# A hybrid MLA and mLSTM layer: the start reordered, sums and products moved from GpSimd to VectorE, the gates' product and two staging tiles moved

## The chip, the cores and the metric

The kernel runs on one core of a Trainium2 chip. The metric is the device time of one execution in microseconds (us). The engines are PE (TensorE, the matrix unit), DVE (VectorE), ACT (ScalarE), POOL (GpSimd) and SP (SyncE, which here only issues transfers). Each engine works through its own list of instructions in order; semaphores make it wait for others.

## The reference

One layer of a diffusion backbone over 128 context and 1024 latent tokens (1152 in all), 1024 features. Cut to what the change touches:

```python
mod = silu(cond) @ w_mod + b_mod              # six vectors: sh1, sc1, gt1, sh2, sc2, gt2
h   = rmsnorm(x, g_norm_mix) * (1 + sc1) + sh1
z   = h @ w_in                                # zq, zkv, zkpe, zmq, zmk, zmv, zgate, zmo, zbr
ckv, kpe = rmsnorm(zkv, g_kv_norm), rope_2d(zkpe)
ig, lf   = zgate + b_gates, log_sigmoid(...)  # input and forget gates of the mLSTM
hm  = bidirectional_mlstm(zmq, zmk, zmv, ig, lf) ; hm = rmsnorm(hm) * sigmoid(zmo)
out = (sigmoid(g_a) * (mla(zq, ckv, kpe) @ w_o_mla) + sigmoid(g_b) * (hm @ w_o_mlstm)) @ w_out
x   = x + gt1 * out ; x = x + gt2 * swiglu(rmsnorm(x) * (1 + sc2) + sh2)
```

Inputs, weights and outputs are fp32.

## The kernel before

Every product is made of three passes in a rounded fp32 format: an operand is split into a high part (ACT, `hi`, L69) and the rest (DVE, `lo`, L75), and `mm3` (L98 to L100) adds high·high, high·low and low·high in PSUM. The big projections use Strassen's seven products in place of eight (`pair`); the sums of weight quarters that these need are made by `w_ops` on the engine `self.G`, the sums of results by `add` (L1716) on DVE. One product of a pair is 24 matmuls of 288 columns.

The instructions are put in order by a scheduler that runs its own timeline; what the code fixes are the data, the buffers, the hints `issue_after`, and how generators are interleaved: `push` appends one, and each product of a pair calls `tick`, which lets it run on to its next `yield`.

The stages that the change touches, with their times in the profiled execution:

- `start` (0 to 155 us). It loads x, the first half of the modulation weights (`wm`, four blocks) and the weights of the mLSTM values (`wv`). `gemv` makes scale and shift of a block; `square` and `stats` make each token's 1/rms, which `stats` spreads to `rbc`; `modk` scales, shifts and splits two features blocks of x. Before that is possible, three of nine token chunks of the value projection V are made from raw x (`rawmm`, L471, in full fp32, which the trace shows as two passes each), with 1/rms and the shift put right afterwards (`shift`, `spread`, L496). Then the other chunks of V follow in groups GA, GB, GC (`vmm`, 512 columns). `copy4` copies the token chunk that straddles two tiles. `t_ops` makes the four differences of x tiles that the Strassen products need.
- `z_lat` and `z_qk` (155 to 345 us): seven pairs. After the second `z_qk`, the generators `krope` and `gates` are pushed: `gates` is a long chain of small instructions on 100 rows (DVE, ACT, and two small PE products, the first at L803).
- `z_big` (345 to 616 us): twelve pairs; their results stand in tiles `zo`, get a sigmoid and are stored to `d_z`. Beside them runs `background`, the second half of the modulation: 64 times one multiply-and-accumulate (DVE, L722), one multiply (L723) and one accumulation (ACT, L704).
- From 616 us `proj` (which needs the tiles `lh`/`ll`, split by the generator `lat_kv` out of loaded pieces `wl`, and stage tiles `st`), then the mLSTM with its loads `neg`, `N`, `S`, `V`, `Q`.

Tiles are taken from numbered places (`slot`, `M`): a new tile in a place must wait until the old one has been used up, its stores included.

Of the kernel before, what the change touches and what calls it, by code (L numbers as in the profile page):

```python
# [10 lines left out]
F32 = mybir.dt.float32  # L11
# [45 lines left out]
class K:  # L57
# [231 lines left out]
    def inputs(self):  # L289

        es = contextlib.ExitStack
        rb, ps, mm = es(), es(), es()
        self.q = []
        self.stores = []
        self.arB = rb.enter_context(self.pool("arB", side="right"))
        for i in range(14):
            self.slot(i, [P, 4, GT], "r")
        self.w2 = es()
        self.wp = self.w2.enter_context(self.pool("w"))
        self.wb = (4, 4)  # L300
        self.G = self.nc.gpsimd
        self.ub = 5
        pp = self.pp = ps.enter_context(self.tc.tile_pool(name="ps1", bufs=1, space=PSUM, reuse_waits="tile"))
        with self.pool("b12") as bp:
            self.hop = {"B12": (bp.tile([P, 4, GT], R32, name="b12h"), bp.tile([P, 4, GT], R32, name="b12l"))}
            with self.pool("s0") as vp:
                self.start(vp)
        self.sp = mm.enter_context(self.pool("u"))
        self.mp = mm.enter_context(self.pool("m"))
        x = lambda nm, g: tuple(t[:, :, g * HT:(g + 1) * HT] for t in self.hop[nm])  # L310
        self.z_lat(x)
        bg = es()
# [12 lines left out]
        bg.close()  # L325
        rb.close()
        ps.close()
        self.z2(mm)

    def start(self, vp):  # L330
# [6 lines left out]
        shs = sp.tile([P, KD, 32], F32, name="shs")  # L337
# [4 lines left out]
        nc.gpsimd.memset(shs, 0.0)  # L342
# [20 lines left out]
        def gemv(b):  # L363
# [16 lines left out]
            nc.vector.tensor_copy(shs[:, 2 * b:2 * b + 2, 0:1], self.mod1[:, 2 * b:2 * b + 2, 1:2])  # L380
# [27 lines left out]
        def stats():  # L408
# [5 lines left out]
            yield r  # L414
# [31 lines left out]
        def copy4(k, j):  # L446
            for e in range(2):
                nc.gpsimd.tensor_copy(c4[:, e, k, 64 * j:64 * j + 64],
                                      self.hop[f"B{k // 4 + 1}{j + 1}"][e][:, k % 4, 0 if j else GT - 64:64 if j else GT])
# [14 lines left out]
        def rawmm(b, sw, e):  # L464

            w = sw.rearrange("p (k f) -> p k f", k=2)
            k = 2 * b + e
            for c in GR:
                if k == 0:
                    ps[c] = self.bank(pp, "mm")  # L470
                nc.tensor.matmul(ps[c], xv(k, 0)[:, c * P:(c + 1) * P], w[:, e], start=k == 0, stop=k == KD - 1)  # L471

        shv = sp.tile([P, 512], F32, name="shv")

        def shift(b):

            g = self.bank(pp, "mx")
            for e in range(2):
                nc.tensor.matmul(g[32 * e:32 * e + 32], shs[:, 2 * b + e], raw[b][:, 512 * e:512 * e + 512], start=True, stop=True)
            if b == 0:  # L480
                nc.scalar.copy(shv[0:64], g[0:64])
            else:
                nc.vector.tensor_add(shv[0:64], shv[0:64], g[0:64])

        def spread():

            sel = sp.tile([64, P], F32, name="selr")
            nc.vector.tensor_scalar(sel, self.ones[0:64], self.vec[0:64, self.V_SEL:self.V_SEL + 1], None, op0=ALU.mult)
            b = self.bank(pp, "mx")
            nc.tensor.matmul(b, sel, shv[0:64], start=True, stop=True)  # L490
            nc.scalar.copy(shv, b)

        def vout(hp, c, r=None, sh=None):
            vs = vp.tile([P, 2 * DV], F32, name=self.nm("vs"), tag="vs", bufs=3)
            if r is not None:
                nc.vector.scalar_tensor_tensor(vs, ps[c], r[:, c:c + 1], sh, op0=ALU.mult, op1=ALU.add)  # L496
            elif c % 2:
                nc.vector.tensor_copy(vs, ps[c])
            else:
                nc.scalar.copy(vs, ps[c])  # L500
            nc.sync.dma_start(self.d_v[c, :, 2 * hp:2 * hp + 2, :], vs.rearrange("p (h v) -> p h v", h=2))
        for b in range(4):
            block(b)
            vload(b)
            xload(b)
        for b in range(4):
            gemv(b)
            sw = f32v(self.wp.tile([P, 4 * DV], R32, name=self.nm("ws"), tag="wo", bufs=self.wb[1]))
            for e in range(2):
                k = 2 * b + e  # L510
                nc.scalar.activation(sw[:, 512 * e:512 * e + 512], raw[b][:, 512 * e:512 * e + 512], AF.Copy, scale=self.A1[:, k, 1:2])
# [7 lines left out]
            raw.pop(b)  # L519
            vload(b + 4)  # L520
        spread()
        for _ in st:
            pass
        for k in range(4):
            modk(k, 1)
        for c in GR:
            vout(0, c, r, shv)
        loadv(4)
        for k in range(4, KD):
            modk(k, 1)  # L530
        c4 = self.slot(13, [P, 2, KD, P], "c4")
        for i in range(4, 12):
            if i > 4:
                vload(i + 3)
            loadv(i + 1)
            for k in (2 * (i % 4), 2 * (i % 4) + 1):
                if i < 8:
                    modk(k, 0)
                    copy4(k, 0)
                    copy4(k, 1)  # L540
                for c in order[i][1]:
                    vmm(wv[i], c, k)
            if i % 4 == 3:
                for c in order[i][1]:
                    vout(1, c)
# [123 lines left out]
    def z_big(self, p, x):  # L669
# [4 lines left out]
        def dst(g):  # L674
            z[g] = self.M((0, 1)[g] if p % 2 else (3, 5)[g], [P, 2, 2, HT], "zo")
# [12 lines left out]
    def background(self):  # L688
# [17 lines left out]
        for i in range(32):  # L706
# [8 lines left out]
            for n in range(2):  # L715
# [7 lines left out]
                nc.gpsimd.tensor_tensor(w[:, n], w[:, n], sr[:, 1], op=ALU.mult)  # L723
# [7 lines left out]
    def krope(self):  # L731
# [17 lines left out]
    def gates(self):  # L749
# [781 lines left out]
    def merge(self):  # L1531
# [43 lines left out]
        self.G = nc.vector  # L1575
# [575 lines left out]
```

## Time and profile before

| what | value |
|---|---|
| three runs | 2160.06, 2153.62, 2159.26 us, median 2159.26 |
| the profiled execution | 2159.8 us, span 2158.0 us |
| granted PE clock, mean of the span | 0.974 |
| busy | PE 95%, DVE 71%, ACT 44%, POOL 24% |
| busy PE of 350 to 600 us | 243.9 of 250 |

PE is the engine that bounds the whole: what counts is where it stands still or does work that could be left out. Three places do so before 650 us: the time until the first product of V with modulated x (65.9 us), the wait in the gates (6.0 us), and the start of `proj` (9.7 us). In the rows, a time is from the span's start; what stands in brackets is the engine's idle time before the instruction and what ended it.

### The profile page before, as it was taken

What the parts mean: (1) busy time and instruction counts of PE and PEld (TensorE: products, weight loads), DVE (VectorE), ACT (ScalarE), POOL (GpSimd) and SP (SyncE); (2) the same over time, 40 slices, a digit from 0 to 9 for tenths busy, and PEclk for the clock granted to TensorE, in tenths of its full rate; (3) what the DMA queues carried; (4) which work ended last, traced back from release to release, by engine and by line L of the source; (5) the groups of instructions that cost most, each with busy time, mean ns of one, the idle gap of its engine ahead of it and who ended that gap; (6) DMA issues with size and microseconds to landing.
All of it is one profiled execution on the core that took longest, in us unless ns stands there. A gap on an engine that the chain in (4) does not pass through costs nothing.

```text
span 2158.0 us, 36478 instructions
## 1 busy us (share of the span) xinstructions
PE 2045.8 (95%) x13495; PEld 1863.7 (86%) x13495; DVE 1540.5 (71%) x3017; ACT 945.6 (44%) x1874; POOL 522.5 (24%) x413
## 2 busy tenths in 40 slices
PE   7899989999989987999999999999999999999997
PEld 3689989989978874666776799999999999999997
DVE  3846756989835878566566476998677766799896
ACT  4533334455445554333443234565323222466564
POOL 0632223667524413344446300000000000000000
PEclk9999999999989998899999999999999999999999
DMA  8332334555479776222225465324555421468664
GB/s 315 105 118 85 115 91 156 171 163 187 147 257 319 250 229 212 68 85 75 69 80 134 128 217 167 123 100 147 188 188 181 157 86 68 140 219 258 220 217 140
DMA packets 233793, 343.87 MB, mean 159 GB/s; under 512 B 20079, under 2 KB 166735, under 8 KB 232463
## 3 DMA queue, kind: packets, MB, share of 16 engines
q1 hardware_dynamic: 225070, 331.88, 47.9%
q0 software_dynamic: 4848, 6.06, 1.1%
q10 hardware_dynamic: 3696, 3.61, 0.5%
q8 instruction: 106, 1.74, 0.3%
q14 instruction: 73, 0.59, 0.1%
HBM read 253.69 MB, written 87.80 MB: 158 GB/s over the span
## 4 chain that ended last, share of the span: by engine, by line
PE 55%; DVE 10%; DMA 9%; issue 3%; ACT 2%; POOL 1%; SPq 1%; DVEq 0%; ACTq 0%; POOLq 0%
PE mm L98 14%; PE mm L100 14%; PE mm L99 13%; PE pv L1477 3%; DMA pr<-w_fo 3%; PE st L98 2%; DVE wo L75 2%; PE st L99 1%; PE st L100 1%; PE mx L1399 1%; DVE sm L1401 1%; DMA wr<-d_w 1%; PE p L1103 1%; POOL wm L723 1%; PE p L1108 1%
## 5 line engine op out<-in xcount | busy, mean ns | idle before, releaser
L98 PE MATMUL mm<-th,wo 128*128 128x288 f32 x1840 | 547.6, 298 | 6.3 <-DVE uu L1716 3.1
L100 PE MATMUL mm<-th,wo 128*128 128x288 f32 x1840 | 542.2, 296 | 4.5 <-DVE wo L75 4.5
L99 PE MATMUL mm<-tl,wo 128*128 128x288 f32 x1840 | 544.9, 296 | 0.0
L98 PEld LDWEIGHTS mm<-th,wo 128*128 128x128 f32 x1840 | 347.3, 189 | 9.1 <-issue 5.0
L100 PEld LDWEIGHTS mm<-th,wo 128*128 128x128 f32 x1840 | 347.3, 189 | 5.9 <-DVE wo L75 5.8
L99 PEld LDWEIGHTS mm<-tl,wo 128*128 128x128 f32 x1840 | 347.8, 189 | 0.1
L75 DVE TENSOR_TENSOR wo<-wr,wo 128x512 fp32r<-128x512 f32 (+1 forms) x317 | 228.2, 734 | 50.8 <-ACT wo L69 47.5
L69 ACT ACTIVATE wo<-wr 128x512 fp32r<-128x512 f32 (+1 forms) x317 | 189.1, 609 | 157.3 <-PE mm L100 71.9
L1943 POOL TENSOR_TENSOR d<-d,rbc 128x576 f32<-128x576 f32 x1 | 1.4, 1394 | 921.5 <-ACT rbc L146 921.5
L69 ACT ACTIVATE wo<-ws 128x512 fp32r<-128x512 f32 x188 | 117.0, 627 | 220.3 <-PE mm L100 201.9
L98 PE MATMUL mm<-xh,wo 128*128 128x288 f32 x616 | 181.8, 296 | 2.0 <-ACT wo L69 2.0
L99 PE MATMUL mm<-xl,wo 128*128 128x288 f32 x616 | 181.6, 296 | 0.8 <-DVE xl L75 0.8
L100 PE MATMUL mm<-xh,wo 128*128 128x288 f32 x616 | 180.1, 295 | 2.2 <-DVE wo L75 2.0
L1446 POOL TENSOR_TENSOR es<-es,p 128x512 f32<-128x512 f32 x112 | 157.3, 1404 | 93.2 <-ACT p L1439 89.4
L1439 ACT ACTIVATE p<-st 128x512 f32<-128x512 f32 (+1 forms) x152 | 87.7, 579 | 157.8 <-PE st L100 146.2
L75 DVE TENSOR_TENSOR wo<-ws,wo 128x512 fp32r<-128x512 f32 x188 | 139.9, 748 | 22.7 <-ACT wo L69 22.5
L1401 DVE TENSOR_REDUCE sm<-mx 128x1 f32<-128x384 f32 (+1 forms) x200 | 99.2, 540 | 67.2 <-PE mx L1399 66.3
L98 PE MATMUL mm<-B,wo 128*128 128x288 f32 x456 | 134.8, 296 | 2.2 <-DVE zo L1716 1.4
L100 PE MATMUL mm<-B,wo 128*128 128x288 f32 x456 | 134.8, 296 | 0.0
L99 PE MATMUL mm<-B,wo 128*128 128x288 f32 x456 | 134.7, 295 | 0.0
L100 PEld LDWEIGHTS mm<-xh,wo 128*128 128x128 f32 x616 | 115.2, 188 | 3.4 <-DVE wo L75 3.4
L98 PEld LDWEIGHTS mm<-xh,wo 128*128 128x128 f32 x616 | 115.5, 188 | 3.0 <-ACT wo L69 3.0
(451 smaller groups left out, 4809.4 us busy)
## 6 DMA issues: line engine op xcount, KB each, us to landing
wr<-w_ff SPq DMA_DIRECT2D x56, 512.0 KB
wm<-wm SPq DMA_DIRECT2D x32, 512.0 KB
wr<-d_w SPq DMA_DIRECT2D x32, 512.0 KB
d_z<-zo SPq DMA_DIRECT2D x48, 288.0 KB
d_g<-uu SPq DMA_DIRECT2D x44, 288.0 KB
wr<-w_big SPq DMA_DIRECT2D x24, 512.0 KB
wr<-w_fo SPq DMA_DIRECT2D x24, 512.0 KB
pr<-w_fo SPq DMA_DIRECT2D x40, 256.0 KB
```

The lines of the kernel that those rows point to most:

```text
L69: i = self.nc.scalar.activation(out, in_, AF.Copy)
L75: return self.nc.vector.tensor_sub(out, in_, f32v(hi)).ins
L98: mm(out, lhs[0], rhs[0], start=first, stop=False, skip_group_check=skip)
L99: mm(out, lhs[0], rhs[1], start=False, stop=False, skip_group_check=skip)
L100: self.pe = mm(out, lhs[1], rhs[0], start=False, stop=last, skip_group_check=skip).ins
L723: nc.gpsimd.tensor_tensor(w[:, n], w[:, n], sr[:, 1], op=ALU.mult)
L1103: self.pe = mm(p1, A[:, h], V[:, h], start=True, stop=not carried).ins
L1108: self.pe = mm(p3, K[:, h], V[:, h], start=True, stop=True).ins
L1401: self.iv = nc.vector.tensor_reduce(sm[:, t, j:j + 1], s[:, :kc], axis=AX.X, op=ALU.max, negate=True).ins
L1439: self.ia = nc.scalar.activation(p[:, :n], st[:, :n], AF.Exp).ins
L1446: nc.gpsimd.tensor_tensor(U["sum"], U["sum"], p, op=ALU.add)
L1477: self.pe = nc.tensor.matmul(pv[g * AV:(g + 1) * AV, q0:q0 + w], v[:, kb[c]], U["P"][c][:, q0:q0 + w], start=c < 2, stop=c == U["nc"] - 1, ...
```

## The change

It has six parts. (a) `start`: all eight loads of x stand ahead of the weights; squares and `stats` come first; the raw products and all that puts them right are gone; each block of x is modulated as soon as its `gemv` is done, and V goes through groups of six and three chunks. (b) `copy4` runs on ACT. (c) the four differences of `t_ops`, (d) the sums of `w_ops` in all nineteen pairs, the 64 multiplies of `background` and three instructions of `krope` run on DVE. (e) the first PE product of `gates` is made six yields later instead of two, and is issued behind the last product. (f) the tiles `zo` of the last two `z_big` pairs are in other places.

```diff
-        self.G = self.nc.gpsimd
+        self.G = self.nc.vector
...
-        GR, GA, GB, GC = (1, 2, 3), (5, 6, 7), (0, 1, 2, 3, 8, 4), (0, 5, 6, 7, 8, 4)
-        order = [(0, GR, kk) for kk in range(4)] + [(hp, g, kk) for hp, g in ((1, GA), (1, GB), (0, GC)) for kk in range(4)]
+        G6, G3 = (0, 1, 2, 3, 5, 6), (7, 8, 4)
+        order = [(hp, g, kk) for hp, g in ((0, G6), (1, G3), (0, G3), (1, G6)) for kk in range(4)]
...
-                nc.gpsimd.tensor_copy(c4[:, e, k, 64 * j:64 * j + 64],
+                nc.scalar.copy(c4[:, e, k, 64 * j:64 * j + 64],
...
-        def rawmm(b, sw, e):
...
-        def shift(b):
...
-        def spread():
...
         for b in range(4):
+            xload(b)
+        for b in range(4):
             block(b)
             vload(b)
-            xload(b)
         for b in range(4):
-            gemv(b)
...
             square(b)
-            rawmm(b, sw, 0)
-            if b == 3:
-                st = stats()
-                r = next(st)
-            rawmm(b, sw, 1)
-            shift(b)
...
+        stats()
+        c4 = None
+        for i in range(12):
+            if i < 4:
+                gemv(i)
+            if i == 0:
+                loadv(0)
+            vload(i + 4)
+            for k in (2 * (i % 4), 2 * (i % 4) + 1):
+                if i < 4:
+                    modk(k, 0)
+                    modk(k, 1)
             loadv(i + 1)
...
                 for c in order[i][1]:
                     vmm(wv[i], c, k)
...
     def t_ops(self, X, xp):
-        G = self.nc.gpsimd
+        G = self.nc.vector
...
-            z[g] = self.M((0, 1)[g] if p % 2 else (3, 5)[g], [P, 2, 2, HT], "zo")
+            z[g] = self.M(((0, 1) if p % 2 and p < 11 else (2, 4) if p == 10 else (3, 5))[g], [P, 2, 2, HT], "zo")
...
-                nc.gpsimd.tensor_tensor(w[:, n], w[:, n], sr[:, 1], op=ALU.mult)
+                nc.vector.tensor_mul(w[:, n], w[:, n], sr[:, 1])
...
-        yield
-        yield
+        for _ in range(6):
+            yield
         ps = self.bank(pp, "mx")
-        nc.tensor.matmul(ps[0:8, 0:18], sel[:, 9:17], SB, start=True, stop=True)
+        with self.tc.issue_after(self.pe):
+            nc.tensor.matmul(ps[0:8, 0:18], sel[:, 9:17], SB, start=True, stop=True)
```

What this does to the order of the instructions is seen at three places. In all rows the number is the row of that engine's list, then the line, the operation, and output<-inputs with the shape; lines of the changed kernel are some 45 lower than those of before.

On PE, at the head of the program. Before, after the first block's modulation (L368, L373), the shift (L479) and the raw products (L471) follow:

```order
1 L368 MATMUL mx_179<-wm_147,sil 32x512 x4
2 L368 MATMUL mx_179<-wm_149,sil 32x512 x4
3 L373 MATMUL mx_190<-vec,rows_188 128x2 x4
4 L479 MATMUL mx_218<-wr_151,shs 32x512 x2
5 L471 MATMUL mm_209<-ws_200,x_17_141 128x512
6 L471 MATMUL mm_211<-ws_200,x_17_141 128x512
7 L471 MATMUL mm_213<-ws_200,x_17_141 128x512
```

Now the sums of squares (L409) and their spreading (L416) come first, then three blocks of modulation weights (L366), then V itself (B and b12h are modulated x, wh and wl the split weights):

```order
1 L409 MATMUL mx_206<-ones,acc_132 128x1 x9
2 L416 MATMUL mx_232<-dg_231,ones 128x128 x4
3 L416 MATMUL mx_243<-dg_242,ones 128x128 x4
4 L416 MATMUL mx_254<-dg_253,ones 128x128
5 L366 MATMUL mx_258<-wm_152,sil 32x512 x4
6 L366 MATMUL mx_258<-wm_154,sil 32x512 x4
7 L371 MATMUL mx_269<-vec,rows_267 128x2 x4
8 L366 MATMUL mx_352<-wm_158,sil 32x512 x4
9 L366 MATMUL mx_352<-wm_160,sil 32x512 x4
10 L371 MATMUL mx_363<-vec,rows_361 128x2 x4
11 L366 MATMUL mx_434<-wm_164,sil 32x512 x4
12 L366 MATMUL mx_434<-wm_166,sil 32x512 x4
```

Row 13 is the first product of V: it stands behind the third block's weights, `wm_166`.

On DVE, from the gates' first instructions before the product to the copy of its result, shortened to where it ends. Before (`g` are the gates' tiles, L1716 sums of a pair's products, `mm_2854` half a product):

```order
293 L799 TENSOR_SCALAR g_2655<-g_2655 100x9
294 L796 COPY g_2655<-g_2655 36x1 x2
295 L799 TENSOR_SCALAR g_2655<-g_2655 100x9
296 L75 TENSOR_TENSOR wo_3000<-wr_2804,wo_3000 128x512
297 L1716 TENSOR_TENSOR u_425_2867<-m_420_2828,mm_2854 128x288
298 L804 COPY g_2655<-mx_2752 8x18
```

Now, with the sums of weights (L1631) in between:

```order
321 L1631 TENSOR_TENSOR ws_3124<-ws_3123,wr_3119 128x512
322 L745 SCALAR_TENSOR_TENSOR g_2679<-g_2679 36x128 x2
323 L751 TENSOR_SCALAR g_2679<-g_2679 100x9
324 L748 COPY g_2679<-g_2679 36x1 x2
325 L751 TENSOR_SCALAR g_2679<-g_2679 100x9
326 L75 TENSOR_TENSOR wo_3011<-wr_2807,wo_3011 128x512
327 L1668 TENSOR_TENSOR u_423_2873<-m_417_2831,mm_2860 128x288
328 L1668 TENSOR_TENSOR u_425_2888<-m_419_2846,mm_2875 128x288
329 L757 COPY g_2679<-mx_2848 8x18
```

The copy has moved behind one more sum of a half product. On PE the gates' product itself was matmul number 1049 among those of 288 columns that follow `start`'s end (1048 before it), and is now behind 1061 of them: 13 later.

On ACT, where `z_big` ends and `proj` begins. Before, the last sigmoid is followed at once by the copies of `proj`'s results; the splits of `lh` are in rows above these:

```order
445 L682 ACTIVATE zo_6273<-zo_6273 128x576
446 L682 ACTIVATE zo_6288<-zo_6288 128x576
447 L897 COPY st_6494<-mm_6495 128x288
448 L897 COPY st_6494<-mm_6503 128x288
449 L897 COPY st_6494<-mm_6517 128x288
```

Now all six splits stand behind the last sigmoid:

```order
477 L634 ACTIVATE zo_6297<-zo_6297 128x576
478 L634 ACTIVATE zo_6312<-zo_6312 128x576
479 L69 ACTIVATE lh_6240<-wl_6244 128x384
480 L69 ACTIVATE lh_6240<-wl_6279 128x384
481 L69 ACTIVATE lh_6240<-wl_6314 128x384
482 L69 ACTIVATE lh_6242<-wl_6353 128x384
483 L850 COPY st_6518<-mm_6519 128x288
484 L69 ACTIVATE lh_6242<-wl_6388 128x384
485 L69 ACTIVATE lh_6242<-wl_6425 128x384
```

The tiles `lh` lie in the place where the last pair's `zo` now lies, so the splits wait until that has been stored. In SP's list, the loads of the last four pieces `wl` and, behind these, of `neg`, `N` and `S` have moved behind the last store of `zo`; the first two pieces are loaded ahead of it.

## Rows read from the trace of the kernel before

**Rows 1.** Busy time by stretch: window and length, then each engine's, clock, DMA share, GB/s.
```profile
0.00:10.00 10.00, 2.38 (x12) 0.60 (x16) 0.28 (x1) 1.50 (x2) 1.35 (x9) 1.00 0.77 280
10.00:20.00 10.00, 8.19 (x25) 3.55 (x18) 1.89 (x7) 5.01 (x8) 0.00 (x0) 1.00 1.02 409
...
65.00:70.00 5.00, 4.10 (x10) 3.27 (x11) 4.00 (x6) 3.95 (x7) 4.03 (x6) 0.50 0.02 4
```
**Rows 2.** PE in order of time, 40 to 68 us: start, length, instruction, idle before.
```profile
47.94 2.31 PE L412 MATMUL mx<-ones,acc 128*128 128x1 f32 x18
...
65.90 0.80 PE L98 MATMUL mm<-wh,b12h 128*128 128x512 f32 x1 [3.32 <-ACT b12h L69]
```
**Rows 3.** PE by line until 66 us: busy us, mean ns of one; idle before.
```profile
L471 PE MATMUL mm<-ws,x 128*128 128x512 f32 x48 | 23.3, 638 | 0.0
```
**Rows 4.** ACT in order of time, 40 to 42 us.
```profile
41.58 1.26 ACT L404 ACTIVATE sqs<-x 128x576 f32<-128x576 f32 x2 [0.26 <-DMA x<-xT]
```
**Rows 5.** PE in order of time, 154 to 155.6 us.
```profile
154.22 0.39 PE L100 MATMUL mm<-wh,B 128*128 128x512 f32 x1
...
155.12 0.29 PE L98 MATMUL mm<-B,wo 128*128 128x288 f32 x1
```
**Rows 6.** ACT by line and shape, 66 to 155 us.
```profile
L69 ACT ACTIVATE B<-x 128x576 fp32r<-128x576 f32 x12 | 8.2, 680 | 0.3
L438 ACT ACTIVATE x<-x,mod 128x448 f32<-128x448 f32 x8 | 5.3, 659 | 0.4 <-DVE x L436 0.4
L438 ACT ACTIVATE x<-x,mod 128x576 f32<-128x576 f32 x6 | 4.7, 776 | 1.9 <-DVE x L436 1.8
...
L438 ACT ACTIVATE x<-x,mod 128x128 f32<-128x128 f32 x8 | 3.2, 397 | 9.1 <-DVE x L436 8.9
```
**Rows 7.** POOL and then DVE in order of time, 84 to 106 us.
```profile
86.78 5.56 POOL L569 TENSOR_TENSOR t<-x,x 128x2304 f32<-128x2304 f32 x1
...
87.84 5.58 DVE L75 TENSOR_TENSOR wl<-wr,wh 128x1024 fp32r<-128x1024 f32 x1
```
**Rows 8.** DVE by line and shape, 1100 to 2150 us, where POOL makes no weight sums.
```profile
L75 DVE TENSOR_TENSOR wo<-wr,wo 128x512 fp32r<-128x512 f32 x204 | 138.8, 691 | 29.1 <-ACT wo L69 28.4
...
L75 DVE TENSOR_TENSOR wl<-wr,wh 128x1024 fp32r<-128x1024 f32 x17 | 20.6, 1223 | 6.4 <-ACT wh L69 6.4
```
**Rows 9.** PE and then DVE in order of time, 300 to 315 us: the gates.
```profile
314.20 0.22 PE L803 MATMUL mx<-g 100*8 100x18 f32 x2 [6.02 <-issue]
...
300.66 0.29 DVE L777 TENSOR_SCALAR g<-g,vec 100x128 f32<-100x128 f32 x1 [1.84 <-DMA g<-d_sp]
...
313.87 0.23 DVE L799 TENSOR_SCALAR g<-g 100x9 f32<-100x9 f32 x1
```
**Rows 10.** Busy time of the stretch 350 to 600 us.
```profile
350.00:600.00 250.00, 243.90 (x1823) 241.62 (x1822) 214.60 (x379) 127.50 (x278) 161.11 (x105) 1.00 0.52 168
```
**Rows 11.** DVE by line and shape, 350 to 600 us.
```profile
L722 DVE SCALAR_TENSOR_TENSOR mj<-wm,sr 128x512 f32<-128x512 f32 x64 | 66.1, 1033 | 8.0 <-ACT sr L711 4.3 <-DMA wm<-wm 3.6
L75 DVE TENSOR_TENSOR wo<-wr,wo 128x512 fp32r<-128x512 f32 x32 | 41.4, 1293 | 9.6 <-ACT wo L69 9.6
L75 DVE TENSOR_TENSOR wo<-ws,wo 128x512 fp32r<-128x512 f32 x43 | 39.6, 921 | 5.7 <-ACT wo L69 5.6
L1716 DVE TENSOR_TENSOR zo<-zo,mm 128x288 f32<-128x288 f32 x66 | 28.1, 442 | 2.6 <-PE mm L100 2.6
```
**Rows 12.** ACT, SP, POOL and PE in order of time, 616 to 642 us.
```profile
627.57 0.70 ACT L897 COPY st<-mm 128x288 f32<-128x288 f32 x2 [9.60 <-DMA d_z<-zo]
...
618.84 0.53 SPq L685 DMA_DIRECT2D d_z<-zo  x1
...
622.94 1.26 POOL L1073 TENSOR_TENSOR N<-N,neg 128x512 f32<-128x512 f32 x1 [2.30 <-DMA N<-d_nm]
...
640.48 0.59 PE L1103 MATMUL p<-V,N 128*128 128x257 f32 x2
```
**Rows 13.** Busy time of the stretch 640 to 650 us.
```profile
640.00:650.00 10.00, 10.00 (x49) 8.81 (x49) 4.74 (x25) 6.96 (x24) 1.38 (x2) 1.00 1.09 353
```

More of the change, by code (lines that the diff above doesn't have):

```diff
@@ L336, in start @@
         sil = sp.tile([P, KD, 32], F32, name="sil")
-        shs = sp.tile([P, KD, 32], F32, name="shs")
         acc = self.slot(1, [P, 2, GT], "acc", F32).rearrange("p j t -> p (j t)")
@@ L341, in start @@
         nc.gpsimd.memset(sil, 0.0)
-        nc.gpsimd.memset(shs, 0.0)
         nc.scalar.dma_start(self.silc, a["cT"])
@@ L379, in gemv @@
                                         self.vec[:, self.V_GMIX + k:self.V_GMIX + k + 1], op0=ALU.add, op1=ALU.mult)
-            nc.vector.tensor_copy(shs[:, 2 * b:2 * b + 2, 0:1], self.mod1[:, 2 * b:2 * b + 2, 1:2])
         nc.scalar.activation(sil[:, :, 0:2], self.silc, AF.Silu)
-        GR, GA, GB, GC = (1, 2, 3), (5, 6, 7), (0, 1, 2, 3, 8, 4), (0, 5, 6, 7, 8, 4)
-        order = [(0, GR, kk) for kk in range(4)] + [(hp, g, kk) for hp, g in ((1, GA), (1, GB), (0, GC)) for kk in range(4)]
+        G6, G3 = (0, 1, 2, 3, 5, 6), (7, 8, 4)
+        order = [(hp, g, kk) for hp, g in ((0, G6), (1, G3), (0, G3), (1, G6)) for kk in range(4)]
         raw, wv = {}, {}
@@ L413, in stats @@
             r = self.rsqrt(st[:, :NCH], NCH, D, sp)
-            yield r
             for c0, n in ((0, 4), (4, 4), (8, 1)):
@@ L447, in copy4 @@
             for e in range(2):
-                nc.gpsimd.tensor_copy(c4[:, e, k, 64 * j:64 * j + 64],
-                                      self.hop[f"B{k // 4 + 1}{j + 1}"][e][:, k % 4, 0 if j else GT - 64:64 if j else GT])
+                nc.scalar.copy(c4[:, e, k, 64 * j:64 * j + 64],
+                               self.hop[f"B{k // 4 + 1}{j + 1}"][e][:, k % 4, 0 if j else GT - 64:64 if j else GT])
         def hc(k, c):
@@ L462, in vmm, with vout @@
             self.mm3(ps[c], hc(k, c), (w[0][:, k % 2], w[1][:, k % 2]), k == 0, k == KD - 1)
-        def rawmm(b, sw, e):
[L466 to L473, printed above, removed]
-        def shift(b):
[L477 to L483, printed above, removed]
-        def spread():
[L487 to L493, printed above, removed]
+        def vout(hp, c):
             vs = vp.tile([P, 2 * DV], F32, name=self.nm("vs"), tag="vs", bufs=3)
-            if r is not None:
-                nc.vector.scalar_tensor_tensor(vs, ps[c], r[:, c:c + 1], sh, op0=ALU.mult, op1=ALU.add)
-            elif c % 2:
+            if c % 2:
                 nc.vector.tensor_copy(vs, ps[c])
@@ L502, in start @@
         for b in range(4):
+            xload(b)
+        for b in range(4):
             block(b)
             vload(b)
-            xload(b)
         for b in range(4):
-            gemv(b)
[L508 to L511, printed above, removed]
-            square(b)
-            rawmm(b, sw, 0)
-            if b == 3:
-                st = stats()
-                r = next(st)
-            rawmm(b, sw, 1)
-            shift(b)
[L519 to L534, printed above, removed]
+            square(b)
+        stats()
[10 more added lines that the diff above has]
+                    modk(k, 1)
             loadv(i + 1)
-            for k in (2 * (i % 4), 2 * (i % 4) + 1):
-                if i < 8:
-                    modk(k, 0)
+            if i == 4:
+                c4 = self.slot(13, [P, 2, KD, P], "c4")
+                for k in range(KD):
                     copy4(k, 0)
                     copy4(k, 1)
+            for k in (2 * (i % 4), 2 * (i % 4) + 1):
                 for c in order[i][1]:
@@ L544, in start @@
                 for c in order[i][1]:
-                    vout(1, c)
+                    vout(order[i][0], c)
         es.close()
@@ L550, in start @@
             hp, g, kk = order[i]
-            vload(i + 3)
+            vload(i + 4)
             for k in (2 * kk, 2 * kk + 1):
@@ L740, in krope @@
         yield
-        nc.gpsimd.tensor_tensor(ka, ka, c0, op=ALU.mult)
-        nc.gpsimd.tensor_tensor(kb, kb, c1, op=ALU.mult)
-        nc.gpsimd.tensor_tensor(ka, ka, kb, op=ALU.add)
+        nc.vector.tensor_mul(ka, ka, c0)
+        nc.vector.tensor_mul(kb, kb, c1)
+        nc.vector.tensor_add(ka, ka, kb)
         yield
@@ L1574, in merge @@
         self.wb = (4, 6)
-        self.G = nc.vector
         ar = es.enter_context(pool("ar"))
```

## The prediction

> **What bounds the kernel now.** I read the busy times of the page first, then windows of 10 us up to 650 us, the groups by line and shape in three stretches, and last the order of time at the places where PE stands. The reader is to see that PE is the bound nearly everywhere (95% of the span), so only three kinds of time can be won: work that PE need not do, time in which it stands, and time at the lower clock. Until 65.90 us PE does no product of V with modulated x [rows 2]; a good third of that, 23.3 us, goes to the 48 passes of raw products [rows 3]. The loads run at 0.409 MB/us after the first 10 us [rows 1], and the last square waits for x until 41.58 us [rows 4], because x is loaded in pieces between the weights. V ends and `z_lat` begins at 155.12 us [rows 5]. In `z_big` PE is busy for 243.9 of 250 us beside a DVE of 214.6 and a POOL of 161.1 [rows 10]: 6.1 us at most are to be had there, and DVE is the next engine in line.
>
> **Start (a, b, c).** What goes is 23.3 us of raw products with shift and spread; what comes is 72 products of V (three chunks, eight features blocks, three passes), since these chunks are now made like the others. The spacing is 0.225 us: four products in 155.12 − 154.22 = 0.90 us [rows 5]. So V has 432 × 0.225 = 97.2 us after its first product.
>
> When is that first product? In PE's list it stands behind the third block of modulation weights. By the shapes of the tiles, x is eight loads of 128 × 1152 fp32 numbers (4.72 MB), a load of `wm` 128 × 2048 (1.05 MB), one of `wv` 128 × 1024 (0.52 MB); up to the third block's second `wm` these are 4.72 + 6 × 1.05 + 2 × 0.52 = 12.06 MB. With 2.8 MB in the first 10 us and 0.409 MB/us after [rows 1] they have landed at 10 + 9.26 / 0.409 = 32.7 us; with the block's own products some 35 us. The other condition is modulated x: x has landed at 14.7 us, the sums of squares at about 17; before, 18.0 us passed from those (47.94) to the first product (65.90) [rows 2], with raw products in between, so 35 us again at the latest. I take 35.3. PE then comes out of a pause: before, the first 5 us ran at a clock of 0.50 [rows 1], the lower level, which costs 2.5 us. So 35.3 + 97.2 + 2.5 = 135.
>
> Cover: per features block ACT needs 0.66 + 0.40 + 0.78 + 2 × 0.68 = 3.2 us [rows 6], 25.6 for eight; the 32 copies of `copy4` have no row on ACT: between nothing and 0.35 us each (half of two copies of 128x288, 0.70 [rows 12]), I take 0.25, 8 us, since they are a quarter as wide. Together 34 us against 32.4 us of PE's first four groups (144 × 0.225), with a head start of some 6 us. It fits narrowly; in ACT's list the copies stand among the modulations of the last four blocks, and what is late is late for PE. I add 3 us (0 to 8) for this and for the result copies between groups: V ends at 138.
>
> The four differences of `t_ops` now cost DVE about 2.75 us each (1.223 us for 1024 columns [rows 8], times 2304/1024), 11 us in the shadow of V. On POOL they took 5.56 us, and the split that began beside one ended with it, 5.58 in place of 1.22 us [rows 7, 8]. So DVE pays nothing net. Gain of the stage: 155 − 138 = 17 us, with bounds of 9 and 20.
>
> **Sums and multiplies on DVE (d).** Between 350 and 600 us POOL does 105 instructions [rows 10], 64 multiplies and 41 weight sums. At 0.691 us, DVE's row for the same shape where POOL makes no sums [rows 8], they add 72.6 us. Against that, DVE's own instructions with two inputs in SBUF are dear now: 1.033, 1.293 and 0.921 us [rows 11] in place of 0.691. If POOL is the reason, 64 × 0.342 + 32 × 0.602 + 43 × 0.230 = 51.1 us go. DVE then has 214.6 + 72.6 − 51.1 = 236 of 250 us: closer to the limit, still under it. The sums from PSUM take 0.442 us [rows 11] and are not dear, which fits, as they read one operand from SBUF. The accumulation on ACT no longer waits for POOL's multiply. PE's 6.1 us of standing: gain 2, with bounds of +6 and, with nothing given back, −70 (below).
>
> The Trainium skill ("SBUF — State Buffer", section "SBUF: two separate sides") calls DVE's second port pair one that it shares with GpSimd under an exclusive lock: who starts first holds it for the whole instruction. By that rule all of the 51 us come back once POOL is silent. The rows of the split beside POOL's difference [rows 7] agree: 5.58 beside 5.56 us. It is why I give the rival of a full DVE a small chance.
>
> **Gates (e).** PE waited 6.02 us for its product, until 314.20; so it came there at 308.2. What it waited for is the chain on DVE that began when `g` had landed, 300.66, and ended at 314.10 [rows 9]: 13.4 us. The change puts PE's product 13 matmuls later; a matmul of 288 columns takes 243.9 / 1823 = 0.134 us [rows 10], so PE comes 1.7 us later. But DVE's list now has three sums of weights inside the chain, up to 3 × 0.69 = 2.1 us. The wait is then 6.0 − 1.7 + 0 to 2.1 = 4.3 to 6.4, I take 5: four more yields move the product by half a product of a pair. Gain 1, bounds −2 (chain longer) and +9 (no wait, and no low clock behind it, about 3 us).
>
> **The last tiles (f).** Before, `proj` began at once, its `lh` being split long before, and stood 9.7 us later because ACT's copy to `st` waited for the store of `zo` in the same place, issued at 618.84, until 627.57 [rows 12]. That wait goes. In its place come six splits of `lh`, which now wait for the last `zo` to be stored: issued at about 618, landing in between nothing and 8.7 us, I take 4 since no load stands ahead in the queue. Of the six pieces only two are loaded by then; `proj`'s first product needs pieces of both features blocks, so a second round of load and split (4 us) lies ahead of it: 626, and a third round for the last columns, 629. So PE's stand is about as long. But `neg`, `N` and `S` stand behind these loads in SP's list: N, which landed at 622.94 [rows 12], comes some 10 us later. The first product of the mLSTM was at 640.48 [rows 12], 17.5 us behind N, of which ACT was held by `st` until after 627.57. So now about 645: loss 5, bounds −2 (gain) and 11, all of the delay, since DMA is full (1.09) from 640 on [rows 13] and cannot catch up quickly.
>
> **Sum.** −17 − 2 − 1 + 5 = −15 against the profiled execution of 2159.8 us, which is 0.5 us from the median of the runs: 2145 us. What follows 650 us is not touched; I leave it.
>
> **Rivals.**
> 1. DVE fills up in `z_big`. If POOL is only half the reason for the dear instructions, 25.6 us come back and the 105 new ones cost about 0.88: 214.6 − 25.6 + 92.4 = 281 for a stretch of 250, so +31; with −17 − 1 + 5 the end is 2178 us. It decides from a DVE load of about 270 of 250 on, where the start's gain is eaten. For it: DVE is already at 214.6 and works in order, so that each wait for ACT's `wo` holds the sums behind it. Against it: the row of 0.691 in 204 instances [rows 8]. If nothing came back, 214.6 + 64 × 1.033 + 41 × 1.1 = 326, and 2160 + 76 − 13 = 2223.
> 2. The gates' wait and low clock go entirely, and `z_big` loses its 6 us: 2160 − 17 − 6 − 9 + 5 = 2133. For it: the stated six yields. Against it: the 13 matmuls.
> 3. The start brings less and the transition costs all: V waits for ACT's copies and for result tiles (V ends at 144), the mLSTM starts 11 us late: 2160 − 11 − 2 − 1 + 11 = 2157. For it: ACT's 34 us against 32, and full DMA behind the transition.
> 4. The transition costs nothing because the mLSTM's loads were early: 2140; this I count with the forecast.
>
> **How the numbers follow.** Forecast, 2138 to 2152, 0.47; rival 2 and others better than 2138, 0.22; rival 3, 2152 to 2165, 0.19; rival 1 and others above 2165, 0.12. A measurement of this kernel tells 0.3%, 6.5 us, from no change: faster is under 2152.8, same up to 2165.7. So faster is 0.47 + 0.22 + 0.02 = 0.71, same 0.17, slower 0.12. The range leaves out a tenth at each end: 2128 to 2164.
>
> **What would show it.** First product of V at 34 to 37 us and `z_lat` at 136 to 142: the start is right; V's spacing above 0.225 with waits for ACT: rival 3. DVE's L75 of 128x512 near 0.69 us in `z_big` and PE busy for over 243 of 250: (d) is right; 0.9 and more, or PE waiting for sums of products: rival 1. A wait of 4 to 6 us of PE in the gates: (e) is as I say; none: rival 2. PE standing twice or three times between the last product of `z_big` and the mLSTM, N landing 7 to 12 us later measured from that last product: (f). The forecast is wrong if the change lies outside these four places, above all if something behind 650 us moves by more than 5 us.

## The result and the profile after

The changed kernel takes 2138.91 us (median of 4 runs, 2138.04 to 2144.58) against 2159.66 of before (four runs): ratio 0.9917, 95% interval 0.9898 to 0.9937. The forecast was 2145 us, range 2128 to 2164. The profiled execution took 2139.5 us with a span of 2137.4; it is read here by the same five places, in us from the span's start (the last column is what the change won between one place and the next):

| place | before | after | won |
|---|---|---|---|
| first product of V with modulated x | 65.90 | 38.24 | |
| first product of `z_lat`: V has ended | 155.12 | 143.46 | 11.7 |
| gates' product | 314.20 | 302.26 | 0.3 |
| last product of `z_big` | 616.46 | 593.16 | 11.4 |
| first product of the mLSTM | 640.48 | 622.44 | -5.3 |
| end of the span | 2158.0 | 2137.4 | 2.6 |

The start, PE in order of time (start, length, instruction, idle before):

```profile
17.52 3.97 PE L409 MATMUL mx<-ones,acc 128*128 128x1 f32 x18 [17.52 <-DVE acc L403]
24.39 4.21 PE L416 MATMUL mx<-dg,ones 128*128 128x128 f32 x18 [2.91 <-DVE dg L415]
...
31.60 1.05 PE L371 MATMUL mx<-vec,rows 128*128 128x2 f32 x8 [0.70 <-ACT rows L368]
...
35.40 1.05 PE L371 MATMUL mx<-vec,rows 128*128 128x2 f32 x8 [0.89 <-ACT rows L368]
36.39 1.92 PE L366 MATMUL mx<-wm,sil 128*32 128x512 f32 x16
38.24 0.50 PE L98 MATMUL mm<-wh,B 128*128 128x512 f32 x1
...
55.42 0.28 PE L371 MATMUL mx<-vec,rows 128*128 128x2 f32 x2
55.63 1.92 PE L366 MATMUL mx<-wm,sil 128*32 128x512 f32 x16
58.44 1.05 PE L371 MATMUL mx<-vec,rows 128*128 128x2 f32 x8 [0.89 <-ACT rows L368]
60.05 0.79 PE L98 MATMUL mm<-wh,B 128*128 128x512 f32 x1 [0.55 <-ACT B L69]
```

The first product of V [rows 2] has come forward by 27.7 us, 2.9 less than I said. Nothing before it waits for weights: the third block's products (36.39) begin without idle time, so PE's own list sets it, which PE works off from 24.39 on with stops of 0.3, 0.7 and 0.9 us, the last two for ACT's copies of the modulation rows. The second half of the rows is a gap that I had not foreseen: from 55.42 to 60.05 PE begins no product of V. It works off the fourth block's modulation, waits for it, and comes back at the lower clock: until 63.4 us a product takes 0.43 us instead of 0.23.

The gates and `z_big`: PE in order of time, then the stretch's busy times, then DVE by line and shape, 340 to 590 us.

```profile
302.26 0.22 PE L756 MATMUL mx<-g 100*8 100x18 f32 x2 [4.07 <-issue]
```
```profile
340.00:590.00 250.00, 250.00 (x1889) 250.00 (x1889) 220.34 (x495) 128.23 (x277) 0.00 (x0) 1.00 0.53 170
```
```profile
L674 DVE SCALAR_TENSOR_TENSOR mj<-wm,sr 128x512 f32<-128x512 f32 x64 | 43.8, 684 | 4.4 <-DMA wm<-wm 3.3 <-ACT sr L663 1.0
L675 DVE TENSOR_TENSOR wm<-wm,sr 128x512 f32<-128x512 f32 x64 | 43.7, 683 | 0.0
L75 DVE TENSOR_TENSOR wo<-ws,wo 128x512 fp32r<-128x512 f32 x44 | 30.2, 686 | 3.0 <-ACT wo L69 2.8
...
L75 DVE TENSOR_TENSOR wo<-wr,wo 128x512 fp32r<-128x512 f32 x33 | 22.6, 685 | 4.6 <-ACT wo L69 4.5
...
L636 DVE TENSOR_SCALAR zo<-zo,vec 128x576 f32<-128x576 f32 x16 | 8.2, 513 | 1.5 <-ACT zo L634 1.5
```

What PE waited for in this stage before (350 to 600 us; line waited for: us in total, times, longest):

```profile
PE mm L100 <- DVE wo L75: 2.7, 4, 1.3
PE mm L98 <- DVE zo L1716: 2.5, 3, 1.2
PE mm L98 <- DVE u L1716: 0.9, 2, 0.4
```

The wait in the gates is 4.07 us [rows 9: 6.02]. PE stands nowhere in `z_big` [rows 10: 6.1 us, for DVE's splits and sums of products], POOL is silent, and every instruction with two inputs in SBUF is back at 0.68 to 0.69 us [rows 11: 0.92 to 1.29].

The transition: PE before, then PE, SP and POOL after, in order of time.

```profile
616.46 0.29 PE L100 MATMUL mm<-th,wo 128*128 128x288 f32 x1
...
628.02 0.61 PE L98 MATMUL mm<-lh,wh 128*128 128x288 f32 x1 [9.67 <-ACT st L897]
```
```profile
593.16 0.29 PE L100 MATMUL mm<-th,wo 128*128 128x288 f32 x1
```
```profile
596.31 1.02 PE L98 MATMUL mm<-lh,wh 128*128 128x288 f32 x2 [2.85 <-ACT lh L69]
599.09 0.61 PE L99 MATMUL mm<-ll,wh 128*128 128x288 f32 x1 [1.77 <-DVE ll L75]
...
606.53 0.61 PE L98 MATMUL mm<-lh,wh 128*128 128x288 f32 x1 [6.11 <-ACT lh L69]
...
622.44 0.60 PE L1056 MATMUL p<-V,N 128*128 128x257 f32 x2
```
```profile
599.06 8.36 SPq L809 DMA_DIRECT2D wl<-d_lat  x4
610.08 0.33 SPq L948 DMA_DIRECT2D neg<-neg  x1
610.51 0.39 SPq L1001 DMA_DIRECT2D N<-d_nm  x1
```
```profile
615.39 2.51 POOL L1026 TENSOR_TENSOR N<-N,neg 128x512 f32<-128x512 f32 x2 [18.08 <-DMA N<-d_nm]
```

Instead of one stand of 9.7 us [rows 12] there are three, together 10.7, and N is issued 17 us behind the last product of `z_big`. The first product of the mLSTM comes 29.3 us behind it, before 24.0. Between the two PE does the same 72 matmuls before and after. The busy times of this stretch, before and after (length, PE busy first, the clock third from the end):

```profile
616.46:640.48 24.02, 13.60 (x76) 13.16 (x74) 5.84 (x7) 9.51 (x26) 13.55 (x19) 0.72 0.95 326
```
```profile
593.16:622.44 29.28, 16.79 (x76) 13.77 (x75) 7.91 (x12) 11.77 (x30) 10.61 (x17) 0.65 0.68 230
```

So the loss of 5.3 us is 2.1 us more of standing (12.5 against 10.4) and 3.2 us more for the same matmuls at a lower clock. N is taken up 22.2 us behind the last product of `z_big`, before 6.5 [rows 12], but PE does not wait for it: the row at 622.44 has no idle time before it.

### The profile page after: what moved, and what is told of

Its sections match the earlier page's. It is cut to its first block, busy times and chain, and to the rows that moved or that the text cites. A ratio compares the mean times of both kernels' runs of the same rounds, so it can differ in the third digit from the quotient of the medians.

```text
span 2137.4 us, 36304 instructions
## 1 busy us (share of the span) xinstructions
PE 2023.3 (95%) x13501; PEld 1864.1 (87%) x13501; DVE 1554.2 (73%) x3159; ACT 948.3 (44%) x1902; POOL 269.8 (13%) x233
## 4 chain that ended last, share of the span: by engine, by line
PE 78%; DMA 8%; DVE 8%; issue 2%; ACT 2%; SPq 1%; POOL 0%; DVEq 0%; ACTq 0%; POOLq 0%
PE mm L98 21%; PE mm L100 21%; PE mm L99 21%; PE pv L1430 3%; DMA pr<-w_fo 3%; PE st L98 2%; PE st L100 2%; PE st L99 2%; PE mx L1352 1%; DVE wo L75 1%; DVE sm L1354 1%; PE p L1056 1%; DMA S<-d_s 1%; PE p L1061 1%; PE p L1058 1%
## 5 line engine op out<-in xcount | busy, mean ns | idle before, releaser
L75 DVE TENSOR_TENSOR wo<-wr,wo 128x512 fp32r<-128x512 f32 (+1 forms) x317 | 206.7, 666 | 47.1 <-ACT wo L69 44.3
L69 ACT ACTIVATE wo<-ws 128x512 fp32r<-128x512 f32 x188 | 117.6, 630 | 258.5 <-PE mm L100 235.7
L75 DVE TENSOR_TENSOR wo<-ws,wo 128x512 fp32r<-128x512 f32 x188 | 128.3, 687 | 15.7 <-ACT wo L69 15.3
```

The costliest lines, as they stand in the source:

```text
L69: i = self.nc.scalar.activation(out, in_, AF.Copy)
L75: return self.nc.vector.tensor_sub(out, in_, f32v(hi)).ins
```

## The experiments

Each is the changed kernel with the edit shown, unless it says "before". Times are medians with the ratio to before (0.9917 for the change). What follows the first mLSTM product is untouched by every edit, yet took 1507 to 1518 us in the profiles, 1515 after the change: a total that moves by less than some 5 us is told by its stage, not by itself. A stage scatters too: in the five profiles with the start of the change V ended between 142.3 and 144.3 us, and took 104.2 to 105.3 us from its first product.

**The multiplies back on POOL.**
```diff
-                nc.vector.tensor_mul(w[:, n], w[:, n], sr[:, 1])
+                nc.gpsimd.tensor_tensor(w[:, n], w[:, n], sr[:, 1], op=ALU.mult)
```


> Changed kernel with the 64 multiplies of background back on POOL, the weight sums staying on DVE. Theory A (instructions of POOL make DVE's two-input instructions wait): POOL is again busy about 100 us in z_big, the split of 128x512 on DVE rises from 0.69 to 0.9 or more, z_big gets longer by 3 to 8 us, total 2142 to 2147. Theory B (POOL delivered the weight sums late, its multiplies did no harm): z_big as in the changed kernel, PE 250 of 250, total 2139.

**The weight sums back on POOL.**
```diff
-        self.G = self.nc.vector
+        self.G = self.nc.gpsimd
...
+        self.G = nc.vector
```
The last line gives the sums behind the mLSTM, which POOL did not make before either, back to DVE.

> Changed kernel with the weight sums of the nineteen pairs back on POOL, the multiplies staying on DVE. Theory A: POOL is busy about 60 us in z_big, so DVE's splits are slowed by a smaller amount, z_big longer by 2 to 5 us, total 2141 to 2144. Theory B: z_big stands for the sums as before, 6 us and more, total 2145 or more; if neither, total 2139. The gates' product should stand after 1049 matmuls of 288 columns again, which tells that the 13 matmuls came from the sums on DVE and not from the yields.

Measured: 2144.56 us (0.9934, 0.9912 to 0.9955) and 2144.36 us (0.9935, 0.9912 to 0.9957). DVE by line, 340 to 590 us, of the first and of the second:

```profile
L674 DVE SCALAR_TENSOR_TENSOR mj<-wm,sr 128x512 f32<-128x512 f32 x64 | 52.4, 818 | 4.0 <-ACT sr L663 3.4 <-DMA wm<-wm 0.4
L75 DVE TENSOR_TENSOR wo<-ws,wo 128x512 fp32r<-128x512 f32 x44 | 34.7, 789 | 5.7 <-ACT wo L69 5.7
L75 DVE TENSOR_TENSOR wo<-wr,wo 128x512 fp32r<-128x512 f32 x32 | 29.6, 925 | 6.6 <-ACT wo L69 6.6
```
```profile
L675 DVE TENSOR_TENSOR wm<-wm,sr 128x512 f32<-128x512 f32 x64 | 53.0, 828 | 0.4
...
L75 DVE TENSOR_TENSOR wo<-ws,wo 128x512 fp32r<-128x512 f32 x44 | 31.1, 706 | 2.3 <-ACT wo L69 2.3
L75 DVE TENSOR_TENSOR wo<-wr,wo 128x512 fp32r<-128x512 f32 x33 | 29.1, 881 | 3.5 <-ACT wo L69 3.5
```

From the gates' product to the last product of `z_big` it took 293.9 and 294.2 us, with the change 290.9. The second number holds 1.6 us of the 12 matmuls by which the gates' product stands earlier there, so the losses are 3.0 and 1.7 us. Theory A stands: with either part on POOL, DVE's instructions are dear again, less than with both, and PE stands again: 2.0 us for DVE's sums of products in the first, 0.7 us for a split in the second (340 to 590 us). B falls: the multiplies alone do harm, and the sums alone cost PE 0.7 us of waiting, not 6. Before, with both, the same stretch cost 9.7 us more (302.3 less 1.7 for 13 matmuls): more than the sum of the two. Why is not shown; a fuller DVE is not the reason, for it was busy for 214.9 of 250 us before and for 221.1 and 224.3 us here.

**Before, with part d alone.**
```diff
-        self.G = self.nc.gpsimd
+        self.G = self.nc.vector
...
-                nc.gpsimd.tensor_tensor(w[:, n], w[:, n], sr[:, 1], op=ALU.mult)
+                nc.vector.tensor_mul(w[:, n], w[:, n], sr[:, 1])
...
```


> Kernel before with part d alone: weight sums of all nineteen pairs, background's multiplies and krope's three instructions on DVE; start, gates, t_ops, copy4 and zo tiles as before. Theory A (POOL's instructions make DVE's two-input instructions wait, and this is what made PE stand in z_big): V ends at 155 us as before, PE busy 250 of 250 in z_big, from the gates' product to the last z_big product 291 us instead of 302, total 2147 to 2151. Rival: the gain of z_big needs the new zo tiles or comes from the gates: total 2154 or more. The gates' product should stand behind 1061 matmuls of 288 columns although the yields are as before, with a wait of 4 us.

Measured: 2147.26 us (0.9946, 0.9929 to 0.9963). Gates' product to the end of `z_big` 291.9 us; the busy times of 350 to 590 us:

```profile
350.00:590.00 240.00, 240.00 (x1815) 240.00 (x1815) 215.37 (x485) 128.48 (x277) 0.00 (x0) 1.00 0.54 175
```

Part d alone brings nearly the whole gain of `z_big`, 10.4 of 11.4 us; new tiles and gates aren't needed. With the two yields of before, the gates' product stands behind 1061 matmuls here, as in the change, and PE waited 4.31 us for it; with the sums on POOL and six yields it stands behind 1049, before behind 1048. So the shorter wait is also the work of d: part e moved the product by one matmul at most.

**Before, with parts a and b alone.** Its diff is that of the change for `start`.

> Kernel before with the new start and copy4 on ACT alone (parts a and b); t_ops, weight sums, multiplies and krope on POOL, gates and zo tiles as before. Expected: first V product at 38 us, V ends 143 to 145 us (12 us gained; up to 2 less than in the changed kernel because t_ops on POOL again holds splits of DVE), gates wait 6 us after 1048 matmuls, z_big as before, total 2146 to 2150. Rival: the start's gain needs t_ops on DVE: V ends at 148 or later, total 2152 or more.

**The differences of `t_ops` back on POOL.**
```diff
     def t_ops(self, X, xp):
-        G = self.nc.vector
+        G = self.nc.gpsimd
```


> Changed kernel with the four differences of t_ops back on POOL (part c undone), nothing else. By the forecast's sum this costs nothing net; by the run of the start alone, where V ended at 151.2 us instead of 143.5, it costs about 7: splits of DVE that begin beside one of the four POOL instructions last about 5 us, PE waits for them some 6 us and runs at the lower clock behind. Theory (lock, in the start): V ends at 149 to 152 us, PE waits for DVE splits 5 to 7 us, total 2144 to 2148. Rival (the later end of the start alone came from the weight sums on POOL): V ends at 143 to 145, total 2138 to 2141.

Measured: 2150.97 us (0.9965, 0.9952 to 0.9977) and 2146.67 us (0.9928, 0.991 to 0.9945). V ended at 151.16 and 151.12 us. PE's waits until 153 us in the second (line waited for: us in total, times, longest), and POOL and DVE in order of time:

```profile
PE mm L100 <- DVE B L75: 4.3, 2, 3.0
...
PE mm L99 <- DVE wl L75: 2.2, 2, 1.7
```
```profile
82.11 5.18 POOL L521 TENSOR_TENSOR x<-x,t 128x2304 f32<-128x2304 f32 x1 [1.43 <-DVE B L75]
87.36 6.03 POOL L521 TENSOR_TENSOR t<-x,x 128x2304 f32<-128x2304 f32 x1
```
```profile
83.23 5.13 DVE L75 TENSOR_TENSOR wl<-wr,wh 128x1024 fp32r<-128x1024 f32 x1 [0.42 <-ACT wh L69]
...
89.49 6.11 DVE L75 TENSOR_TENSOR wl<-wr,wh 128x1024 fp32r<-128x1024 f32 x2
```

A split of 1.23 us takes 5.13 us and ends 1.07 us behind POOL's instruction beside it (88.36 against 87.29), as if it had stood until that was over; PE waits for such splits, 6.5 us in all. So of the 11.7 us of the start 7.7 hang on part c; a and b alone win 4.0. What c alone would win on the old start was not run; the kernel before has one such wait too, 3.65 us at 104.91. My expectation of the start alone (V's end at 143 to 145) was wrong by that: V's end is the rival's, the total lies between the two forecasts.

**`copy4` back on POOL.**
```diff
-                nc.scalar.copy(c4[:, e, k, 64 * j:64 * j + 64],
+                nc.gpsimd.tensor_copy(c4[:, e, k, 64 * j:64 * j + 64],
```


> Changed kernel with the 32 copies of copy4 back on POOL (part b undone), nothing else. On ACT each copy took 0.15 to 0.24 us (5 us in all) between modulations that PE waits for little. Theory: the copies on ACT cost PE nothing, and on POOL, where one takes 0.3 to 0.8 us with one SBUF input, they hold few splits: V ends within 1.5 us of 143.5, total 2138 to 2141. Rival: the copies read SBUF on POOL and hold DVE's splits and multiplies of x (two inputs) in the stretch 57 to 71 us: V ends 2 to 5 us later, total 2141 to 2145.

Measured: 2133.93 us (0.9876, 0.9858 to 0.9894); V ended at 141.53 us. PE's wait for ACT's split `B` at 60.05 is gone, and so is the low clock behind the gap. Busy times of 60 to 65 us with this edit, of the changed kernel, and of the kernel with the multiplies on POOL, whose start is that of the change (the clock is the third number from the end); last, PE's first product of V behind the gap in that kernel:

```profile
60.00:65.00 5.00, 5.00 (x23) 4.14 (x23) 5.00 (x13) 4.72 (x9) 5.00 (x10) 1.00 0.37 108
```
```profile
60.00:65.00 5.00, 4.95 (x15) 3.97 (x16) 3.58 (x8) 5.00 (x19) 0.00 (x0) 0.67 0.37 108
```
```profile
60.00:65.00 5.00, 4.82 (x20) 3.65 (x21) 3.56 (x7) 5.00 (x19) 0.00 (x0) 1.00 0.33 108
```
```profile
60.00 0.50 PE L98 MATMUL mm<-wh,B 128*128 128x512 f32 x1 [0.55 <-ACT B L69]
```

The third has the wait of the change and yet the full clock: of the five profiles with this start three show the low clock behind the gap and two do not. From its first product V takes 102.8 us with this edit, 104.4 us in the third kernel and 105.2 in the change. Neither theory had that: part b costs V some 1.5 us, and the other 0.9 us are the low clock, which the copies are not shown to bring. The other 3 us of the total lie behind 620 us and are within the scatter.

**The four `gemv` calls ahead of the loop.**
```diff
-            if i < 4:
-                gemv(i)
             if i == 0:
+                for b in range(4):
+                    gemv(b)
                 loadv(0)
```


> Changed kernel with the four gemv calls made ahead of the loop over value blocks instead of one in each of the first four turns. In the changed kernel PE reaches the last piece of the third block's modulation (L371) only at 55.42 us, behind the second block's products, and V stands or does the fourth block until 60.05, then runs at the lower clock to 63.4; ACT and DVE are idle for 6.5 and 5.5 us before. Theory: this order costs V some 5 us; expected first V product 38 us, no gap at 55 to 60, V ends 138 to 140 instead of 143.46, total 2134 to 2137. Rival: ACT and DVE, not PE's order, set the pace of blocks three and four (modulation and the 32 copies): the gap moves but V ends within 1.5 us of 143.5, total 2138 to 2140.

Measured: 2135.79 us (0.989, 0.9872 to 0.9908); V ended at 141.04 us. The gap at 55 to 60 us is gone, PE has no wait after its first product of V. But of the gap 3.2 us were work (0.28 + 1.92 + 1.05) and are still done, spread out; only the waits and the low clock were to be won. V's end moved by 2.4 us, between the two forecasts; from its first product V takes 102.3 us.

**Twelve yields in the gates.**
```diff
-        for _ in range(6):
+        for _ in range(12):
```


> Changed kernel with 12 yields instead of 6 ahead of the gates' first product; in the order of PE it then stands behind 1104 matmuls of 288 columns (43 later than now, 5.7 us of PE's time). Theory: the chain on DVE ends at the same time, so the wait of 4.07 us and the low clock behind it (13 matmuls at 0.24 us, 1.4 us) go: total 2133 to 2135. Rival: the rest of the gates' chain moves back too and its second product or the stores of its results (used by neg, N, S) become late: PE waits at the second product or before the mLSTM, total 2138 to 2141.

Measured: 2131.93 us (0.9872, 0.9854 to 0.989). PE in order of time:

```profile
304.61 0.21 PE L756 MATMUL mx<-g 100*8 100x18 f32 x2
...
310.25 0.31 PE L768 MATMUL mx<-g 8*100 8x9 f32 x2 [0.35 <-DVE g L763]
```

No wait at the first product and 0.35 us at the second, and from V's end to the end of `z_big` 444.5 us instead of 449.7: 5.2 us, the 4.07 of the wait and the low clock behind it. So the wait that part e touches can go, with more yields than it has. The first mLSTM product came 31.3 us behind `z_big`, 2.0 later than in the change, as the rival would have it; with the old `zo` tiles (the three edits below) nothing of that is seen.

**The `zo` tiles in their old places.**
```diff
-            z[g] = self.M(((0, 1) if p % 2 and p < 11 else (2, 4) if p == 10 else (3, 5))[g], [P, 2, 2, HT], "zo")
+            z[g] = self.M((0, 1)[g] if p % 2 else (3, 5)[g], [P, 2, 2, HT], "zo")
```


> Changed kernel with the zo tiles of the last two z_big pairs in their old places (part f undone), nothing else. Theory: the transition to proj cost the change 5.3 us (first mLSTM product 17.7... us after the last product of z_big before the change was 23.9, now 29.2), because the splits of lh wait for the stores of zo and the loads of wl, neg, N, S stand behind. Expected: lh is split before z_big ends, PE stands about 9.7 us for st as before the change, the first mLSTM product comes 23 to 25 us after the last z_big product, total 2133 to 2135 us. Rival: the mLSTM is limited by its transfers, and what is won at its start is lost until the first zq product: total within 2 us of 2139.

Measured: 2131.2 us (0.9875, 0.9856 to 0.9895); first mLSTM product 23.4 us behind the last product of `z_big`, not 29.3. Part f cost 5.9 us; the rest of the 7.7 is in the scatter. Over all profiles the distance is 29.3 to 31.3 us with the new places (seven kernels) and 21.7 to 24.4 with the old ones (seven).

**Three edits together: old `zo` tiles, early `gemv`, twelve yields.**

> Changed kernel with three edits together: zo tiles of before (measured alone 2131.2), the four gemv calls ahead of the loop (measured alone 2135.8, 3.1 less than the changed kernel), 12 yields in the gates. If the three gains add up: 2131.2 - 3.1 - 4 to 5.5 = 2122.6 to 2124. Rival: the wait for st at the head of proj or the mLSTM's transfers take part of it back: 2126 to 2130.

Measured: 2124.28 us (0.9843, 0.9824 to 0.9862). The gains add up within the scatter. V ends at 140.8, `z_big` at 585.1 us.

**The same, with the last pair's two tiles exchanged.**
```diff
-            z[g] = self.M((0, 1)[g] if p % 2 else (3, 5)[g], [P, 2, 2, HT], "zo")
+            z[g] = self.M(((1, 0) if p == 11 else (0, 1) if p % 2 else (3, 5))[g], [P, 2, 2, HT], "zo")
```


> The kernel of the three edits (zo tiles of before, early gemv, 12 yields; measured 2124.3) with one more: the two zo tiles of the very last z_big pair change places (1, 0 in place of 0, 1), so that the half that is stored first lies where proj's first stage tile st goes. Theory: the copy to st waited 9.4 us because the half stored last, behind neg, N and S, lay in its place; now the first st waits at most 2 us, the second stage tile, needed some 30 matmuls later, waits for that late store for up to 5 us. First mLSTM product 16 to 19 us after the last z_big product instead of 21.7, total 2118 to 2122. Rival: the mLSTM's start is set by its transfers, not by st: first product 21 us or more behind, total 2123 to 2126.

Measured: 2126.19 us (0.9838, 0.9821 to 0.9854). PE in order of time, its waits in the transition:

```profile
588.22 0.40 PE L98 MATMUL mm<-lh,wh 128*128 128x288 f32 x1 [1.39 <-ACT st L850]
596.70 0.61 PE L98 MATMUL mm<-lh,wh 128*128 128x288 f32 x1 [4.28 <-ACT st L850]
```

Up to the first mLSTM product PE's waits for `st` fell from 9.4 to 6.4 us, and yet that product stayed 21.7 us behind. The number is the rival's, its reason is not shown: in PE's order 84 matmuls of `proj` now stand ahead of that product instead of 72, and these 12 take up the 3 us. PE waits 0.7 us for S (POOL) and 1.1 us for N's product with S (DVE), but only at 628 and 636 us. The total is not to be told from that of the three edits.

**Three edits, with `copy4` on POOL.**

> The kernel of the three edits (zo tiles of before, early gemv, 12 yields; measured 2124.3) with copy4 on POOL as before the change. In the changed kernel this moved the end of V from 143.46 to 141.53 us. Theory: ACT's copies delay the splits of modulated x also here; V ends at 138.5 to 140 us instead of 140.83, total 2121 to 2124. Rival: with the early gemv ACT has time for the copies and V already runs without a wait; V ends within 0.7 us of 140.8, and the total differs only by what the untouched rest of the program scatters (4 us).

Measured: 2123.11 us (0.9822, 0.98 to 0.9843). V ended at 140.53 us against 140.83: with the early `gemv` the copies cost nothing on either engine. Not to be told from the three edits; both beat before and change.

## Why the prediction was right, and where not

The direction, the range and the sum hold (15 us forecast, 20.7 measured), but that the total came so near is in part luck: the start brought 5.3 us less than forecast, the sums and multiplies some 7 more, and 2.6 came from the rest, which nothing touched.

- **Start, 17 forecast, 11.7 measured.** Two terms were too small. "With the block's own products some 35 us": the weights were there in time, PE's serial list of sums, spreading and three blocks with their copies was the last condition: 38.24. From there to V's end the sum had 97.2 + 2.5 + 3, and it took 105.2 us. It left out PE's own work on the third and fourth blocks' modulation, some 4 us, which stands among the products of V; with the `gemv` calls ahead and no wait at all V still took 102.3. The rest is waits (1.4 us) and the low clock (1.6 us), which came behind the gap and not at the first product, where I had put 2.5 us for it: there the products are 0.23 us apart. It was visible only in part: PE's order shows the fourth block behind the second's products. "DVE pays nothing net" for `t_ops` held, as PE waits for no split in the change, but it treated the busy time of DVE; what counted was that PE waits for the very split that POOL holds. On that hang 7.7 of the 11.7 us, so the new order of the start itself was worth 4.0. The split in [rows 7] did not end with POOL's instruction either: it began and ended 1.1 us behind it, and the like lengths, 5.58 and 5.56, are chance.
- **Sums and multiplies, 2 forecast, about 9 measured.** From the gates' product to the end of `z_big` 11.4 us were won; 1.7 are the 13 matmuls done earlier, and 0.8 the shorter low clock (13 matmuls at 0.24 us instead of 21). The mechanism was right, DVE's instructions came back to 0.69 us. But DVE's load rose to 220, not 236. The scaling of `zo` (L636) fell to 0.513 us too, which I had not counted: 8.7 us. And I added whole lengths, while DVE's instructions overlap: the lengths of its rows add up to 253.6 us where it was busy for 220.3 (before, 235.7 and 214.6). In the start alone, where POOL works as before, the scaling took:

```profile
L636 DVE TENSOR_SCALAR zo<-zo,vec 128x576 f32<-128x576 f32 x16 | 16.9, 1056 | 0.8 <-ACT zo L634 0.8
```

  The Trainium skill ("SBUF — State Buffer", section "Who interferes with whom") lists `tensor_scalar` among the operations that can take the shared pair; 1.056 against 0.513 us agrees. PE then waited for nothing, so all of its 6.1 us went where I had taken 2 of them; for the other 2.7 us of the 9 no wait of PE accounts.
- **Gates, 1 forecast.** The wait was 4.07 us, just below the 4.3 to 6.4. The 13 matmuls were right, their cause was not: they come from the sums on DVE, not from the yields. The three sums did stand inside the chain, yet it lasted 13.0 us (289.17 to 302.16), not 13.4 to 15.5: its own instructions got shorter with POOL silent, the last two scans (L793, now L745) from 1.77 to 0.86 us in all.
- **Last tiles, 5 lost forecast, 5.3 measured.** The stands hold: three of PE for `lh` and `ll`, together about as long as the one before. The step from N to the mLSTM failed: N was taken up 15.7 us later than before, not 7 to 12, and PE did not wait for it. The loss is 2.1 us more of standing in `proj` and 3.2 us of lower clock, which the sum did not have; that 5 met 5.3 is luck.
- **Rivals.** DVE did not fill up; the low clock behind the gates stayed. Rival 3 was right on V's end (144, measured 143.46), rival 2 on the 6 us of `z_big`; in the total they nearly cancel. Of the signs, the first product of V (34 to 37), `z_lat` (136 to 142) and N were missed. The untouched rest gave 2.6 us, within what it scatters.

## What to carry to other kernels

Where the instructions of one engine hold up those of another, as GpSimd's did VectorE's here, look for the split or sum that the matrix engine is waiting for and ask what runs beside it: four instructions of GpSimd that no busy share would show cost 7.7 us here. Before trusting a hint in the code (a yield, an order hint), count in the finished order what stands in front of the instruction: six yields moved next to nothing, twelve removed the wait. When a buffer moves, list both what the old place kept waiting and what the new one will.

## What the hardware showed that I had not expected

A `tensor_scalar` of 128x576 with one tensor from SBUF halves its mean time (1.056, single ones 0.51 to 1.55, to 0.513 us) when POOL is silent, while sums with one operand from PSUM keep theirs (0.442 before, 0.447 after). And two copies of 128x64 took ACT 0.39 us, while single ones took POOL 0.23 to 1.46 us beside a working DVE. A wait of PE need not bring the lower clock: behind the same gap with the same wait of 0.55 us the granted clock over 5 us was 0.66 to 0.67 in three profiles and 1.00 in two.
